# RWKV inverse on one core: the block products of both tiles of a batch taken phase by phase instead of tile by tile

## Chip, cores and metric

One core of a Trainium2 chip. The metric is the device time of one execution in microseconds, as the median over runs; the kernel before was timed three times (1305.89, 1308.43 and 1310.21 us, median 1308.43).

## What is computed

One decoder layer with three token mixers (Mamba-2 SSD, S5, RWKV-7) that read one input projection, are gated, merged, projected and normalised. Batch 1, 256 tokens, model width 2048, all float32.

```python
proj = jnp.einsum('bsd,dc->bsc', x, w_in[l]).astype(jnp.float32)
y_a = mamba2_branch(...)          # SSD, 32 heads
y_b = s5_branch(...)              # complex diagonal scan
y_c = rwkv7_branch(...)           # 16 heads of 64 channels
gates = jax.nn.sigmoid(p_gate.reshape(b, s, N_BRANCHES, d) + gate_b[l])
merged = gates[:, :, 0] * (y_a @ w_branch_a[l]) + gates[:, :, 1] * (y_b @ w_branch_b[l]) + gates[:, :, 2] * (y_c @ w_branch_c[l])
x = layer_norm(DEEPNORM_ALPHA * x + merged @ w_out[l], ln_g[l], ln_b[l])
# inside rwkv7_branch, for every token t and head:
state = state * w_t[:, :, None, :] + sa[..., None] * b_t[:, :, None, :] + v_t[..., None] * k_t[:, :, None, :]
y_t = jnp.einsum('bhvk,bhk->bhv', state, r_t)      # sa = state @ a_t
```

## The kernel before

Every projection is done to nearly float32 precision by splitting both factors in a high and a low part (fp32r): per block of 128 input channels three matmuls of 128x256, `xhi*hi`, `xlo*hi` and `xhi*lo` (lines 417 to 419 for the input projection, 1234 to 1236 for the branches, 863 to 865 and 1337 to 1339 with 512 columns). They are called weight matmuls here. Each weight tile is loaded by DMA, rounded to `hi` on ScalarE (L344), and `lo = raw - hi` is made on VectorE (L346). These weight matmuls stream through TensorE for nearly the whole kernel, and everything else on TensorE is put between them in small groups. Such a group, from the last weight matmul before it to the first one after it, is called a visit.

The RWKV recurrence is done in chunks of 64 tokens, 4 chunks, for 4 batches of 2 tiles of 2 heads each (`b` 0 to 3; tile `i`, head `h`, chunk `c`). Each chunk needs the inverse of a 64x64 unit triangular matrix. Its two 32x32 diagonal blocks are inverted on VectorE (`rwkv_tinv`, L676 and L677, 31 column steps) and go through DRAM into `TTf` (L685). The off-diagonal block is made from them by two products, and this is the part that the change touches:

- `rwkv_ty1` (L698) transposes one diagonal block of both tiles, 16 matmuls of 32x32, into PSUM tiles `py`.
- `rwkv_ty2` copies it to `Y` on ScalarE (L709), multiplies by `Aoff` (L712), copies (L713), multiplies by the other diagonal block (L716), and copies the result into `TTf` (L717). It does so tile by tile, and inside a tile half by half: L712 of one head, its copy, L712 of the other head, its copy, then the same with L716. `Y` has one buffer.
- `rwkv_chunks` then walks the 4 chunks of a batch in order: L731 (a product that needs no inverse), copy, L735 (multiplies by `TTf`), copy, L741, L744 and L747.

A float32 matmul is two instructions in the trace, so a group of 4 matmuls of 32x32 is eight there.

The program order is written in two lists of steps (`PROG`: `T` is the diagonal inverse, `Y` the products, `C` the chunks; `PROG2` after it, with `S` an SSD group and `s` an S5 tile). A scheduler that simulates the engines makes from it the fixed order of instructions on each engine; a step whose inputs come earlier is placed earlier. SSD group work touched below: L924 and L927 are the two matmuls of the state tile `st`, with the ScalarE copy `ST` (L926) between them, and L942 is the product `y`. S5: L1143 makes `s5pk`, ScalarE copies it in four pieces (L1147), and L1195 (`s5y`) uses the copy; L1173 makes `s5bu`.

Of the kernel before, what the change touches and what calls it, by code (L numbers as in the profile page):

```python
# [8 lines left out]
F32 = mybir.dt.float32  # L9
F32R = mybir.dt.float32r  # L10
AF = mybir.ActivationFunctionType
# [193 lines left out]
def emit(tc, I, O, parts=("rwkv", "s5", "ssd", "final"), dbg=None):  # L205
    nc = tc.nc
    ctx = ExitStack()
    with ctx:
# [23 lines left out]
        for st in PROG:  # L232
            if st[0] in "FAB":
                b = int(st[1:])
                if st[0] != "B":
                    bts[b] = rwkv_keys(g, b)
                if st[0] != "A":
                    rwkv_front(g, bts[b], b)
            elif st[0] == "T":
                rwkv_tinv(g, bts[int(st[1:])], int(st[1:]))  # L240
            elif st[0] == "Y":
                b = int(st[1:])
                with tc.high_priority() if b in BEHIND else ExitStack():
                    with tc.issue_after(g.mms[BEHIND[b][0]][BEHIND[b][1]].ins) if b in BEHIND else ExitStack():
                        py = rwkv_ty1(g, bts[b], b)
                    rwkv_ty2(g, bts[b], b, py)
            elif st[0] == "C":
                with tc.high_priority() if int(st[1:]) in BEHIND else ExitStack():
                    rwkv_chunks(g, bts[int(st[1:])], int(st[1:]))
            elif st[0] == "g":  # L250
                gate_c(g, int(st.split("_")[1]))
            elif st[0] == "z":
                rwkv_z(g, int(st[1:]))
            else:
                s5_u(g, int(st[1:]))
# [188 lines left out]
NCH = T // CL  # L444
# [217 lines left out]
def rwkv_tinv(g, bt, b):  # L662

    nc, rp = g.nc, g.rp
    AT = rp.tile([128, 32, 32], F32, name=f"AT{b}", tag="AT")
    TT = rp.tile([128, 8, 32], F32, name=f"TT{b}", tag="TT")
    Pm = rp.tile([128, 8, 32], F32, name=f"Pm{b}", tag="Pm")
    src = bt.Ad.rearrange("i c h q s t -> (i c h q) s t")
    for cs in range(4):
        nc.sync.dma_start(AT[32 * cs:32 * cs + 32], src)  # L670
    nc.sync.dma_start(TT.rearrange("p c i -> p (c i)"), g.I["tti"])
    nc.gpsimd.memset(AT.rearrange("p s t -> p (s t)")[:, ::33], 1.0)  # L672
    for i in range(1, 32):
        n = i + 1
        col = AT[:, 0:n, i].unsqueeze(1).to_broadcast([128, 8, n])
        nc.vector.tensor_tensor(Pm[:, :, 0:n], TT[:, :, 0:n], col, ALU.mult)  # L676
        nc.vector.tensor_reduce(TT[:, :, i], Pm[:, :, 0:n], AX.X, ALU.add)  # L677
    for cs in range(4):
        r = slice(32 * cs, 32 * cs + 32)
        nc.sync.dma_start(bt.Td[:, cs], TT[r])  # L680
    td = bt.Td.rearrange("(m h q) u c i -> m h q (u c) i", h=2, q=2)
    for h in range(2):
        for q in range(2):
            r0 = 64 * h + 32 * q
            nc.sync.dma_start(bt.TTf[r0:r0 + 32, h].rearrange("s i c t -> s (i c) t")[:, :, 32 * q:32 * q + 32],  # L685
                              td[:, h, q].rearrange("m c i -> c m i"))


HS = [(slice(64 * h, 64 * h + 32), slice(64 * h + 32, 64 * h + 64)) for h in range(2)]
# [11 lines left out]


def rwkv_ty2(g, bt, b, pys):
    nc, rp = g.nc, g.rp
    for i in range(2):
        py = pys[i]
        Y = rp.tile([128, 2, NCH, 32], F32, name=f"Yl{b}_{i}", tag="Yl", bufs=1)
        for lo, hi in HS:
            nc.scalar.activation(Y[lo, 0], py[lo, 0], AF.Copy)  # L709
        for lo, hi in HS:  # L710
            for c in range(NCH):
                nc.tensor.matmul(py[hi, 1, c, :], lhsT=bt.Aoff[lo, i, c, :], rhs=Y[lo, 0, c, :], start=True, stop=True)  # L712
            nc.scalar.activation(Y[hi, 1], py[hi, 1], AF.Copy)  # L713
        for h, (lo, hi) in enumerate(HS):
            for c in range(NCH):
                nc.tensor.matmul(py[lo, 2, c, :], lhsT=Y[hi, 1, c, :], rhs=bt.TTf[hi, h, i, c, 32:64], start=True, stop=True)  # L716
            nc.scalar.activation(bt.TTf[lo, h, i, :, 32:64], py[lo, 2], AF.Copy)  # L717


def rwkv_chunks(g, bt, b):  # L720
# [669 lines left out]
```

## Time and profile before

| | |
|---|---|
| median of 3 runs | 1308.43 us (1305.89 to 1310.21) |
| the profiled execution | 1302.54 us, span of the instructions 1300.6 us |
| granted TensorE clock, mean | 0.997 |
| TensorE matmul busy | 1268.7 us (98%) |
| VectorE busy | 995.7 us (77%) |
| ScalarE busy | 768.5 us (59%) |

The profiled execution is 5.9 us below the median of the runs. "Busy" for TensorE means that some matmul was in flight; it doesn't say that the matmuls stood as close as they can, so a visit that spreads them out is inside the 98%.

### The profile page before, as it was taken

Reading aid. Unit: us, or ns where it says so; the run is one execution under the profiler, and the core shown is the slowest. Engines: PE = TensorE matmul, PEld = TensorE weight load, DVE = VectorE, ACT = ScalarE, POOL = GpSimd, SP = SyncE. Lnnn points to the kernel's source line nnn. Section 1 sums busy time; section 2 is a strip of 40 time slices with the busy share of each in tenths; the row PEclk is TensorE's granted clock in tenths of the full one; section 3 lists DMA queues with packets and bytes.
Section 4 is the critical chain, followed back from the end, with each engine's and each line's share of the span. In section 5 each row is a group of like instructions: output and inputs, shape, how many; then the busy total and the mean of one; then the engine's idle time right before and its main releaser. Section 6 shows DMA issues by size and latency. Waiting matters only on the chain.

```text
span 1300.6 us, 27378 instructions
## 1 busy us (share of the span) xinstructions
PE 1268.7 (98%) x10916; PEld 1195.2 (92%) x10916; DVE 995.7 (77%) x1823; ACT 768.5 (59%) x1379; POOL 14.8 (1%) x72
## 2 busy tenths in 40 slices
PE   8999999999999999989999999999999999999996
PEld 8999999999989889889989989999999999999885
DVE  6779987669959857889999867999597565448655
ACT  6676555577555657885756766766454454444530
POOL 2000000000000000000000000000000000000000
PEclk9999999999999999999999999999999999999998
DMA  8655655444564554555555556456655656677751
GB/s 313 181 169 173 187 174 167 139 124 145 166 177 152 168 183 132 159 186 164 178 163 180 170 178 195 146 158 192 193 171 164 193 179 211 209 230 243 255 167 65
DMA packets 97039, 230.71 MB, mean 177 GB/s; under 512 B 26736, under 2 KB 41616, under 8 KB 96912
## 3 DMA queue, kind: packets, MB, share of 16 engines
q1 hardware_dynamic: 96336, 227.60, 57.1%
q8 instruction: 86, 1.41, 0.5%
q10 hardware_dynamic: 576, 1.36, 0.3%
q14 instruction: 41, 0.34, 0.1%
HBM read 224.37 MB, written 3.24 MB: 175 GB/s over the span
## 4 chain that ended last, share of the span: by engine, by line
PE 80%; DVE 7%; ACT 6%; DMA 3%; issue 2%; SPq 1%; DVEq 0%; POOL 0%; ACTq 0%; POOLq 0%
PE ps_g L418 6%; PE ps_g L417 6%; PE ps_g L419 6%; PE br L1235 4%; PE br L1234 4%; PE br L1236 4%; PE ps_x L417 3%; PE ps_x L418 3%; PE ps_x L419 3%; PE po L1337 2%; PE po L1338 2%; PE po L1339 2%; PE zq L865 2%; PE zq L864 2%; PE zq L863 2%
## 5 line engine op out<-in xcount | busy, mean ns | idle before, releaser
L417 PE MATMUL ps_g<-xhi,hi_g 128*128 128x256 f32 x768 | 215.2, 280 | 0.0
L418 PE MATMUL ps_g<-xlo,hi_g 128*128 128x256 f32 x768 | 215.1, 280 | 0.0
L419 PE MATMUL ps_g<-xhi,lo_g 128*128 128x256 f32 x768 | 213.8, 278 | 0.0
L346 DVE TENSOR_TENSOR lo_g<-raw_g,hi_g 128x1024 fp32r<-128x1024 f32 x96 | 117.5, 1224 | 66.6 <-ACT hi_g L344 61.9
L344 ACT ACTIVATE hi_g<-raw_g 128x1024 fp32r<-128x1024 f32 x96 | 101.5, 1058 | 93.8 <-PE ps_g L418 71.4
L418 PEld LDWEIGHTS ps_g<-xlo,hi_g 128*128 128x128 f32 x768 | 144.6, 188 | 2.0 <-issue 1.0
L417 PEld LDWEIGHTS ps_g<-xhi,hi_g 128*128 128x128 f32 x768 | 144.6, 188 | 0.9
L417 PE MATMUL ps_x<-xhi,hi_x 128*128 128x256 f32 x512 | 144.6, 282 | 0.6 <-ACT sq L950 0.6
L419 PEld LDWEIGHTS ps_g<-xhi,lo_g 128*128 128x128 f32 x768 | 144.2, 188 | 0.5
L418 PE MATMUL ps_x<-xlo,hi_x 128*128 128x256 f32 x512 | 143.9, 281 | 0.0
L419 PE MATMUL ps_x<-xhi,lo_x 128*128 128x256 f32 x512 | 143.6, 280 | 0.0
L344 ACT ACTIVATE hi_b<-raw_b 128x1024 fp32r<-128x1024 f32 x64 | 67.8, 1059 | 75.8 <-PE br L1235 43.9
L346 DVE TENSOR_TENSOR lo_x<-raw_x,hi_x 128x1024 fp32r<-128x1024 f32 x64 | 78.3, 1223 | 27.1 <-ACT hi_x L344 27.1
L417 PEld LDWEIGHTS ps_x<-xhi,hi_x 128*128 128x128 f32 x512 | 96.3, 188 | 1.6 <-ACT sq L950 0.8
L419 PEld LDWEIGHTS ps_x<-xhi,lo_x 128*128 128x128 f32 x512 | 96.3, 188 | 0.9 <-issue 0.2
L418 PEld LDWEIGHTS ps_x<-xlo,hi_x 128*128 128x128 f32 x512 | 96.3, 188 | 0.7 <-issue 0.2
L346 DVE TENSOR_TENSOR lo_b<-raw_b,hi_b 128x1024 fp32r<-128x1024 f32 x64 | 78.8, 1231 | 21.6 <-ACT hi_b L344 19.6
L344 ACT ACTIVATE hi_x<-raw_x 128x1024 fp32r<-128x1024 f32 x64 | 67.5, 1055 | 39.7 <-PE ps_x L418 23.2
L1234 PE MATMUL br<-yh0h,hi_b 128*128 128x256 f32 x256 | 72.0, 281 | 0.7 <-DVE sg L1297 0.7
L1235 PE MATMUL br<-yh0l,hi_b 128*128 128x256 f32 x256 | 72.3, 283 | 0.0
L1236 PE MATMUL br<-yh0h,lo_b 128*128 128x256 f32 x256 | 71.7, 280 | 0.0
L676 DVE TENSOR_TENSOR Pm<-TT,AT 128x16 f32<-128x16 f32 (+30 forms) x124 | 50.8, 410 | 11.6 <-POOL AT L672 5.8
(446 smaller groups left out, 3872.9 us busy)
## 6 DMA issues: line engine op xcount, KB each, us to landing
raw_g<-in_wt SPq DMA_DIRECT2D x96, 512.0 KB, 4.4
raw_x<-in_wt SPq DMA_DIRECT2D x64, 512.0 KB, 4.2
raw_za<-in_wza SPq DMA_DIRECT2D x32, 512.0 KB, 3.8
raw_b<-in_wba SPq DMA_DIRECT2D x32, 512.0 KB, 4.5
raw_wo<-in_wout SPq DMA_DIRECT2D x32, 512.0 KB, 4.7
raw_k<-in_wt SPq DMA_DIRECT2D x16, 512.0 KB, 4.8
raw_r<-in_wt SPq DMA_DIRECT2D x16, 512.0 KB, 4.1
raw_v<-in_wt SPq DMA_DIRECT2D x16, 512.0 KB, 3.8
```

The lines of the kernel that those rows point to most:

```text
L344: nc.scalar.activation(hi, raw, AF.Copy)
L346: nc.vector.tensor_tensor(lo, raw, hi.bitcast(F32), ALU.subtract)
L417: m.append(nc.tensor.matmul(ps, lhsT=hi.k(k), rhs=g.xhi[:, k, :], start=(k == 0), stop=False))
L418: m.append(nc.tensor.matmul(ps, lhsT=hi.k(k), rhs=g.xlo[:, k, :], start=False, stop=False))
L419: m.append(nc.tensor.matmul(ps, lhsT=lo.k(k), rhs=g.xhi[:, k, :], start=False, stop=(k == NK - 1)))
L676: nc.vector.tensor_tensor(Pm[:, :, 0:n], TT[:, :, 0:n], col, ALU.mult)
L863: nc.tensor.matmul(ps[tk], lhsT=g.xhi[:, kk, t], rhs=hi.k512(k), start=f0, stop=False)
L864: nc.tensor.matmul(ps[tk], lhsT=g.xhi[:, kk, t], rhs=lo.k512(k), start=False, stop=False)
L865: nc.tensor.matmul(ps[tk], lhsT=g.xlo[:, kk, t], rhs=hi.k512(k), start=False, stop=l0)
L1234: nc.tensor.matmul(ps, lhsT=hi.k(k0 + k), rhs=h, start=(k == 0), stop=False)
L1235: nc.tensor.matmul(ps, lhsT=hi.k(k0 + k), rhs=l, start=False, stop=False)
L1236: nc.tensor.matmul(ps, lhsT=lo.k(k0 + k), rhs=h, start=False, stop=(k == n - 1))
```

## The change

`rwkv_ty2` takes both tiles through each phase together: the copies of `Y` for both, all 16 matmuls of the first product, the four copies, all 16 of the second product, the four copies. The two heads alternate inside a phase. The second tile's `Y` gets a buffer of its own, from the ring `sq2` of two buffers that the z step (`zt`, L783) and the chunk's tail (`ysq`, L766) use. No matmul or copy is added or removed. Lines after L717 move by 6 (L731 becomes L737, L735 L741, L924 L930, L927 L933, L942 L948, L1143 L1149, L1173 L1179, L1195 L1201); L712 becomes L713, L713 becomes L716, L716 becomes L720 and L717 becomes L723.

```diff
 def rwkv_ty2(g, bt, b, pys):
+
     nc, rp = g.nc, g.rp
+    Ys = [rp.tile([128, 2, NCH, 32], F32, name=f"Yl{b}_{i}", tag=("Yl", "sq2")[i], bufs=1 + i) for i in range(2)]
     for i in range(2):
-        py = pys[i]
-        Y = rp.tile([128, 2, NCH, 32], F32, name=f"Yl{b}_{i}", tag="Yl", bufs=1)
         for lo, hi in HS:
-            nc.scalar.activation(Y[lo, 0], py[lo, 0], AF.Copy)
+            nc.scalar.activation(Ys[i][lo, 0], pys[i][lo, 0], AF.Copy)
+    for i in range(2):
+        for c in range(NCH):
+            for lo, hi in HS:
+                nc.tensor.matmul(pys[i][hi, 1, c, :], lhsT=bt.Aoff[lo, i, c, :], rhs=Ys[i][lo, 0, c, :], start=True, stop=True)
+    for i in range(2):
         for lo, hi in HS:
-            for c in range(NCH):
-                nc.tensor.matmul(py[hi, 1, c, :], lhsT=bt.Aoff[lo, i, c, :], rhs=Y[lo, 0, c, :], start=True, stop=True)
-            nc.scalar.activation(Y[hi, 1], py[hi, 1], AF.Copy)
+            nc.scalar.activation(Ys[i][hi, 1], pys[i][hi, 1], AF.Copy)
+    for i in range(2):
+        for c in range(NCH):
+            for h, (lo, hi) in enumerate(HS):
+                nc.tensor.matmul(pys[i][lo, 2, c, :], lhsT=Ys[i][hi, 1, c, :], rhs=bt.TTf[hi, h, i, c, 32:64], start=True, stop=True)
+    for i in range(2):
         for h, (lo, hi) in enumerate(HS):
-            for c in range(NCH):
-                nc.tensor.matmul(py[lo, 2, c, :], lhsT=Y[hi, 1, c, :], rhs=bt.TTf[hi, h, i, c, 32:64], start=True, stop=True)
-            nc.scalar.activation(bt.TTf[lo, h, i, :, 32:64], py[lo, 2], AF.Copy)
+            nc.scalar.activation(bt.TTf[lo, h, i, :, 32:64], pys[i][lo, 2], AF.Copy)
```

The scheduler makes a new order from this. ScalarE, batch 2, from the first copy of `Y` on, before (`py_0` and `Yl_0` are tile 0's; tile 1's copies stand in the same pattern behind these rows):

```order
L709 ACTIVATE Yl_0_4896<-py_0_4878 32x128 x2
L344 ACTIVATE hi_u_1_5479<-raw_u_1_5477 128x1024
L560 ACTIVATE acc_248<-ps_g_10_5359,hgb 128x256
L832 ACTIVATE ea<-par 32x1
L713 ACTIVATE Yl_0_4896<-py_0_4878 32x128
L344 ACTIVATE hi_u_0_5535<-raw_u_0_5533 128x1024
L713 ACTIVATE Yl_0_4896<-py_0_4878 32x128
L344 ACTIVATE hi_u_1_5541<-raw_u_1_5539 128x1024
L971 ACTIVATE yb<-ps_u_5421 128x128x2
L815 ACTIVATE dtu<-dtx 32x256
L816 ACTIVATE dtu<-dtu 32x256
L717 ACTIVATE TTf_2625<-py_0_4878 32x4x32
```

The same place after the change:

```order
L709 ACTIVATE Yl_0_4896<-py_0_4878 32x128 x2
L709 ACTIVATE Yl_1_4897<-py_1_4887 32x128 x2
L344 ACTIVATE hi_u_0_5473<-raw_u_0_5471 128x1024
L716 ACTIVATE Yl_0_4896<-py_0_4878 32x128 x2
L716 ACTIVATE Yl_1_4897<-py_1_4887 32x128 x2
L344 ACTIVATE hi_u_1_5479<-raw_u_1_5477 128x1024
L560 ACTIVATE acc_248<-ps_g_10_5359,hgb 128x256
L723 ACTIVATE TTf_2625<-py_0_4878 32x4x32 x2
L723 ACTIVATE TTf_2625<-py_1_4887 32x4x32 x2
```

Both tiles' copies now stand together, and no copy of a tile waits behind the other tile's products.

TensorE, batch 1, the first product, as a piece of the difference (weight matmuls of a z tile around it):

```order
+L713 MATMUL py_0_2560<-Yl_0_2578,Aoff_1160 32x32 x8
 L419 MATMUL ps_z_3466<-xhi,lo_z_0_3458 128x256
 L417 MATMUL ps_z_3466<-xhi,hi_z_0_3456 128x256
 L418 MATMUL ps_z_3466<-xlo,hi_z_0_3456 128x256
 L419 MATMUL ps_z_3466<-xhi,lo_z_0_3458 128x256
+L713 MATMUL py_1_2569<-Yl_1_2579,Aoff_1160 32x32 x8
```

In batches 1 and 3 the first product is thus two visits, four weight matmuls apart; in batches 0 and 2 it is one, and the second product (L720) is one in all four.

TensorE, SSD group 2 (an early step of `PROG2`), before (`st` is the group's state; L927, its second matmul, follows thirteen weight matmuls after the last row):

```order
L924 MATMUL st_7324<-xdec_7322,BT_7306 128x256
L418 MATMUL ps_x_7452<-xlo,hi_x_0_7442 128x256
L419 MATMUL ps_x_7452<-xhi,lo_x_0_7444 128x256
L417 MATMUL ps_x_7452<-xhi,hi_x_0_7442 128x256
L418 MATMUL ps_x_7452<-xlo,hi_x_0_7442 128x256
L419 MATMUL ps_x_7452<-xhi,lo_x_0_7444 128x256
L942 MATMUL y_7344<-xdt_7315,csb_2_7298 128x64 x4
L942 MATMUL y_7344<-xdt_7315,csb_2_7300 128x64 x4
```

The same group after the change:

```order
L930 MATMUL st_7324<-xdec_7322,BT_7306 128x256
L948 MATMUL y_7344<-xdt_7315,csb_2_7298 128x64 x4
L948 MATMUL y_7344<-xdt_7315,csb_2_7300 128x64 x4
L1149 MATMUL s5pk_7822<-s5cq_7798,s5W_7793 32x32 x8
L1179 MATMUL s5bu_0_7886<-s5U_7784,s5WT_7820 128x128 x3
L933 MATMUL st_7324<-ST_7326,C_7139 128x256
L1179 MATMUL s5bu_0_7886<-s5U_7784,s5WT_7820 128x128
L1201 MATMUL s5y_7918<-yb,s5k_5882 128x128
```

The first S5 tile's work has come forward into the same visit, and no weight matmul stands between the two matmuls of `st`, nor between `s5pk` and `s5y`.

## Rows read from the trace of the kernel before

**Rows 1.** The page: busy time of each engine, and the chain by engine.

```profile
PE 1268.7 (98%) x10916; PEld 1195.2 (92%) x10916; DVE 995.7 (77%) x1823; ACT 768.5 (59%) x1379; POOL 14.8 (1%) x72
...
PE 80%; DVE 7%; ACT 6%; DMA 3%; issue 2%; SPq 1%; DVEq 0%; POOL 0%; ACTq 0%; POOLq 0%
```

**Rows 2.** Waits of TensorE: waiting line and releaser; us in total, times, longest us.

```profile
PE yT L959 <- ACT y L955: 4.1, 5, 1.3
PE py L698 <- DMA TTf<-Td: 4.1, 4, 1.7
...
PE st L927 <- ACT ST L926: 2.7, 1, 2.7
PE chy L744 <- ACT SVA L737: 1.8, 1, 1.8
...
PE s5pb L1137 <- DVE yb L1201: 0.2, 1, 0.2
```

**Rows 3.** TensorE in order of time, a lone visit of eight (start us, us).

```profile
170.84 0.28 PE L417 MATMUL ps_r<-xhi,hi_r 128*128 128x256 f32 x1
...
171.18 0.28 PE L417 MATMUL ps_r<-xhi,hi_r 128*128 128x256 f32 x1
171.38 0.43 PE L712 MATMUL py<-Yl,Aoff 32*32 32x32 f32 x8
171.75 0.39 PE L418 MATMUL ps_r<-xlo,hi_r 128*128 128x256 f32 x1
...
172.33 0.28 PE L419 MATMUL ps_r<-xhi,lo_r 128*128 128x256 f32 x1
```

**Rows 4.** TensorE in order of time, the 32 instructions of L698 in one visit.

```profile
236.92 0.28 PE L418 MATMUL ps_k<-xlo,hi_k 128*128 128x256 f32 x1
237.13 0.69 PE L698 MATMUL py<-cst,TTf 32*32 32x32 f32 x32
237.75 0.39 PE L419 MATMUL ps_k<-xhi,lo_k 128*128 128x256 f32 x1
...
238.32 0.28 PE L417 MATMUL ps_k<-xhi,hi_k 128*128 128x256 f32 x1
```

**Rows 5.** TensorE in order of time, a visit shared with a chunk's product.

```profile
181.67 0.28 PE L419 MATMUL ps_g<-xhi,lo_g 128*128 128x256 f32 x1
181.87 0.45 PE L731 MATMUL ch<-SVA,XS 128*64 128x64 f32 x8
182.25 0.43 PE L712 MATMUL py<-Yl,Aoff 32*32 32x32 f32 x8
182.62 0.38 PE L417 MATMUL ps_g<-xhi,hi_g 128*128 128x256 f32 x1
...
183.19 0.28 PE L418 MATMUL ps_g<-xlo,hi_g 128*128 128x256 f32 x1
```

**Rows 6.** TensorE in order of time, one matmul of L735 as a visit.

```profile
195.33 0.28 PE L418 MATMUL ps_g<-xlo,hi_g 128*128 128x256 f32 x1
195.53 0.33 PE L735 MATMUL ch<-X,TTf 128*64 128x64 f32 x2
195.79 0.38 PE L419 MATMUL ps_g<-xhi,lo_g 128*128 128x256 f32 x1
...
196.13 0.28 PE L418 MATMUL ps_g<-xlo,hi_g 128*128 128x256 f32 x1
```

**Rows 7.** ScalarE's copies by line: duration ns min/median/max, first and last start.

```profile
L709 ACT ACTIVATE Yl<-py x16: 249/268/269, 164.1 to 465.8; 32x128 f32<-32x128 f32 x16
...
L1147 ACT ACTIVATE s5k<-s5pk x32: 168/188/190, 600.5 to 990.8; 32x32 f32<-32x32 f32 x32
```

**Rows 8.** Stretches: length, then PE, PEld, DVE, ACT, POOL busy us, PEclk, DMA share, GB/s.

```profile
480.00:520.00 40.00, 38.87 (x381) 36.74 (x382) 30.16 (x57) 29.37 (x69) 0.00 (x0) 1.00 0.51 158
...
560.00:600.00 40.00, 34.36 (x288) 33.42 (x286) 38.90 (x119) 29.93 (x55) 0.21 (x2) 1.00 0.49 154
```

**Rows 9.** ScalarE in order of time, ahead of the copy `ST` at 565.90.

```profile
564.07 1.28 ACT L937 ACT_TABLE_LOAD   x1
```

## The prediction

> **What bounds the kernel now.** I read the page first. TensorE is busy 98% of the span, VectorE 77%, ScalarE 59%, and the chain of work that ended last runs through TensorE for 80% of the span [rows 1]. Next, TensorE's own waits. There are 13 of them and they add up to 21.4 us, the largest two 4.1 us each [rows 2]. So of 1300.6 us TensorE stands still for under 2%. It is the bound, and what can be gained in quantity is either those 21 us or work of TensorE itself. The third view, TensorE in order of time, shows where its own time can be lost without a wait. In a plain stretch the weight matmuls start 0.113 us apart (three steps from 170.84 to 171.18) [rows 3]. A visit of small matmuls breaks this pace by more than its own arithmetic, and that is the quantity the change works on.
>
> **What a visit costs.** Take the last weight matmul before the visit and the fifth after it: five steps at 0.113 would be 0.567 us. Around a lone L712 group of eight they are 172.33 - 171.18 = 1.15, so the visit costs 0.58 us [rows 3]. Around 32 instructions of L698 they are 238.32 - 236.92 = 1.40, so it costs 0.83 us [rows 4]; with the odd hundredth that still lags behind I take 0.85. Four times the matmuls cost 0.27 us more: most of a visit is its fixed part. Where L712 shares the visit of a chunk's product the two together cost 183.19 - 181.67 - 0.57 = 0.95 [rows 5]; with 0.58 for one of them, sharing costs about 0.38. A single matmul of L735 alone costs, over four steps, 196.13 - 195.33 - 0.34 = 0.46, say 0.47 [rows 6].
>
> **The change, part by part.**
>
> Removed: by the order, the products of L712 and L716 are 32 groups of eight before, eight per batch. 19 of them are visits of their own and 13 share one with other small work: 19 x 0.58 + 13 x 0.38 = 16.0 us. Beside that, in every batch the first L735 is torn into three pieces, since the second tile's inverse comes late; three pieces at 0.47 against one whole visit of 0.58 is 0.8 us, four times 3.3 us. Together 19.3 us.
>
> Added: six full visits of 32 (four L720, two L713) and, in batches 1 and 3, the first product in two visits of 16 instructions each, which lie between 0.58 and 0.85; I take 0.67. That is 6 x 0.85 + 4 x 0.67 = 7.8 us. One L731 in batch 0 is torn in two instead (2 x 0.47 - 0.58 = 0.4). Together 8.2 us. **The visits save 19.3 - 8.2 = 11 us**, all on TensorE and so on the path.
>
> The price of a full visit is the one unknown here, since no L712 or L716 group of 32 exists. From below it is L698's 0.83, the nearest row: the same 32x32 shape, 32 instructions, both heads alternating as the new loops do. From above it is four groups that each pay the price of sharing, 0.20 + 4 x 0.38 = 1.7 us, as if nothing overlapped; then two halves cost 0.96 each, the added part is 14.4 us, and 5 us are saved. I take the lower one. Against it stands a rule of the Trainium skill (TensorE: Matmul & The Clock Gate, section "Wait — 56ns, not 53.3ns?"): start-to-start of matmuls never drops below about 25 ns, however few columns they have. By an estimate from that page a visit of 32 would be at least 31 x 9 ns = 0.28 us dearer than I say and six of them 1.7 us. The trace doesn't agree: 32 instructions, each 0.19 us long, fit in 0.69 us, which is 16 ns apart [rows 4].
>
> Copies: sixteen of each kind, each about 0.27 us [rows 7], are the same number on ScalarE as before, now four in a row. TensorE's next phase waits for four instead of one or two: 4 x 0.27 = 1.1 us. In the order 21 to 29 weight matmuls, 2.4 us or more, stand ahead of each phase; only behind the second half of the first product in batches 1 and 3 they are 16 and 18, and its own two copies take 0.54. So nothing is added there while those weight matmuls are ready; without them each of the eight phases would show 1.1 us. One more table load on ScalarE (42 for 41, 1.28 us [rows 9]) lies beside other work. Rounding of weights that is queued on ScalarE behind a copy waits for the visit at most once per phase rather than twice per tile; it has slack (59%).
>
> Moved: the end of the chunks. Counted in weight matmuls, the last chunk's matmuls of batch 0 move from about 1625 to 1511, of batch 1 from 2079 to 1825, of batch 3 from 3447 to 3152, so at 0.113 us each 13, 29 and 33 us earlier. No TensorE work disappears with that; it only frees VectorE and ScalarE work of the recurrence to be done earlier, and pulls S5's first tile forward (its first matmul from weight matmul 3830 to 3662). From 480 to 520 us VectorE is busy 30.2 of 40 us, from 560 to 600 it is 38.9 of 40, and there TensorE has only 34.4 [rows 8]. DMA issues are the same in number; the four groups that carry the inverse through DRAM move with it on SP's queue, and weight loads behind them have not held TensorE so far (no weight load is among the waits of rows 2).
>
> Waits: the one I expect to get longer is at SSD group 2. There ScalarE's copy `ST` came 2.7 us late once [rows 2], behind table loads of 1.28 us [rows 9], although 18 weight matmuls (2.0 us) stood between the two matmuls of `st`. In the new order none stand there, and four copies of 0.19 us [rows 7] also lie uncovered between `s5pk` and `s5y` in the same visit. Bounds: nothing, if other work in that visit or an earlier ScalarE covers it; 2.7 + 2.0 + 0.8 = 5.5 us. I take 3. Of the other waits I drop half of the 1.8 us before L744 [rows 2], since its place and ScalarE's order both change. Net **2 us more waiting**.
>
> Sum: -11 + 2 = -9 us. The profiled execution would go from 1302.5 to 1293.5; it stands 5.9 us below the median of the runs shown, so for the median I say 1308.4 - 9.4, or 1299.
>
> **The rivals.** (1) The early end of the chunks also takes waits away. For it: the stretch from 560 us, where VectorE is full and TensorE loses 5.6 us [rows 8], gets its S5 work earlier out of a stretch with 10 us of idle VectorE. Against it: the new order itself packs S5's tile into one visit with group 2. If all of those 5.6 us and the 1.8 go, and the visit at group 2 is covered, it is 1308.4 - 11 - 7.4 = 1290. (2) The visits are worth less: full visits near 1.7 us, or phases that wait for their four copies, 8 x 1.1 us. Saved 5 us, less 2 of waiting: 1305, which is no change. For it: the operands come from SBUF places that ScalarE has only just written; against it: L698 also multiplies blocks that have just arrived, at 0.83. (3) Slower: the one visit of group 2 and S5's first tile becomes a long halt. Six dependent steps stand in it without a weight matmul, and TensorE takes its instructions in order, so everything waits for the latest of `ST`, `s5k` and the S5 weights, and all three are made by ScalarE. It decides from 15 us on, since it must eat the 11 us and 4 more. ScalarE would need about four table loads (5.1 us) and ten instructions of 1 us ahead of them; before, the halt at this copy was 2.7 us. At 18 us it gives 1308 - 11 + 18 = 1315. (4) That the change doesn't do what it says is excluded by the order for the second product, and half true for the first in batches 1 and 3, which is in the sum.
>
> **How the numbers follow.** A measurement of this kernel tells about 0.3%, 3.9 us, from no change. My forecast has 0.62, rival 1 0.13, rival 2 (with forecasts in which the waits eat most of the gain) 0.17, rival 3 0.08. So faster 0.75, within 0.3% 0.17, slower 0.08. The range runs from rival 1 (1290) to forecasts with visits at 1.7 us and the full 5.5 us of waiting, 1308.4 - 5 + 5.5 = 1309; I give 1289 to 1309.
>
> **What would show it.** Right: L713 and L720 as groups of 32 (two of 16) with the fifth weight matmul about 1.4 us behind the last one before; L741 whole in every first chunk; the chunks' last matmuls of batch 3 some 30 us earlier; sum of TensorE's waits near 23 us. Wrong: a full visit over 1.2 us; L713 or L720 waiting for L709 or L716 by name; a wait at `st`, `s5y` or `s5bu` of over 5 us; or waits that sum to over 30 us.

## The result and the profile after

| | before | after |
|---|---|---|
| median | 1308.57 us (1305.89 to 1310.21, 4 runs) | 1294.45 us (1293.05 to 1295.61, 4 runs) |
| profiled execution | 1302.54 us, span 1300.6 | 1294.02 us, span 1292.0 |
| granted TensorE clock, mean | 0.997 | 0.992 |

The ratio is 0.9894, with a 95% interval of 0.9874 to 0.9913: 14.1 us faster, between 11.4 and 16.5. The two profiled executions are only 8.5 us apart. The text below takes these two differences apart.

The page of after, its first lines on the engines, the granted clock in 40 slices, and the chain by engine:

```profile
PE 1264.8 (98%) x10916; PEld 1193.6 (92%) x10916; DVE 994.7 (77%) x1823; ACT 769.0 (60%) x1380; POOL 15.0 (1%) x72
...
PEclk9999989999999999899999999999999999999999
...
PE 87%; DVE 5%; ACT 3%; DMA 2%; issue 2%; SPq 1%; ACTq 0%; DVEq 0%; POOL 0%; POOLq 0%
```

The same instructions ran on TensorE, 10916, and it is busy 3.9 us less than in [rows 1]. It is still the bound. Its share of the chain rose from 80% to 87%, that of VectorE and ScalarE fell from 13% to 8%. The two slices with an 8 in the clock row are new; they come up again below.

The visits first. TensorE of after in order of time (start us, us): a second product with all 32 instructions in one visit, batch 0.

```profile
173.48 0.28 PE L419 MATMUL ps_r<-xhi,lo_r 128*128 128x256 f32 x1
173.69 0.69 PE L720 MATMUL py<-TTf,Yl 32*32 32x32 f32 x32
174.31 0.39 PE L417 MATMUL ps_r<-xhi,hi_r 128*128 128x256 f32 x1
...
174.77 0.28 PE L417 MATMUL ps_r<-xhi,hi_r 128*128 128x256 f32 x1
```

Over four steps it costs 174.77 - 173.48 - 4 x 0.113 = 0.84 us, as L698 does in [rows 4], and all four L720 visits lie between 0.840 and 0.843. The same view in batch 1 shows the first product in its two halves:

```profile
226.68 0.28 PE L418 MATMUL ps_z<-xlo,hi_z 128*128 128x256 f32 x1
226.89 0.44 PE L713 MATMUL py<-Yl,Aoff 32*32 32x32 f32 x16
...
227.93 0.44 PE L713 MATMUL py<-Yl,Aoff 32*32 32x32 f32 x16
...
228.75 0.28 PE L417 MATMUL ps_z<-xhi,hi_z 128*128 128x256 f32 x1
```

From 226.68 to 228.75 there are eight steps of weight matmuls, so the two halves cost 2.07 - 0.91 = 1.16 us, 0.58 each. Sixteen alternating instructions cost no more than a lone eight (0.58 in [rows 3]).

Waits of TensorE, after (waiting line and releaser; us in total, times, longest us):

```profile
PE zq L870 <- DVE lo_za L346: 3.6, 1, 3.6
PE warm L360 <- ACT zero L358: 3.2, 1, 3.2
PE py L698 <- DMA TTf<-Td: 2.3, 2, 1.2
PE py L713 <- ACT Yl L709: 1.5, 1, 1.5
PE yT L965 <- ACT y L961: 1.4, 1, 1.4
...
PE zq L869 <- ACT hi_za L344: 0.9, 1, 0.9
...
```

With those under 0.15 us, which the view leaves out, they add up to 16.7 us, against 21.5 of before. The 2.7 us at `st` behind `ST` and the 1.8 us before L744 are gone [rows 2], and so are three waits of the branch matmuls (L1234, 3.1 us together in before); `yT` fell from 4.1 to 1.4 and L698 from 4.1 to 2.3. L713 with 1.5 us and a `ps_u` matmul with 1.0 are new, and `zq` rose from 0.4 to 4.5 us.

The three stretches behind the end of the chunks, by windows (us, then busy time and count of PE, PEld, DVE, ACT and POOL, granted clock, DMA share, GB/s), after:

```profile
480.00:520.00 40.00, 39.29 (x327) 38.44 (x326) 35.67 (x74) 29.36 (x56) 0.00 (x0) 1.00 0.61 179
520.00:560.00 40.00, 35.48 (x188) 30.05 (x187) 30.81 (x101) 26.88 (x41) 0.11 (x1) 0.91 0.45 136
560.00:600.00 40.00, 39.10 (x342) 37.93 (x341) 39.21 (x84) 29.82 (x68) 0.32 (x3) 1.00 0.63 189
```

The last chunk matmul (L747, now L753) starts at 479.2 us instead of 527.0, and VectorE's idle time from 480 us is used: 35.7 us busy for 30.2 [rows 8]. TensorE's 5.6 idle us from 560 us are down to 0.9. But the stretch ahead of it, which had none in before, now has 4.5.

### The profile page after: what moved, and what is told of

It reads as the page before. It is cut to its first block, busy times and chain, and to the rows that moved or that the text cites. A ratio compares the mean times of both kernels' runs of the same rounds, so it can differ in the third digit from the quotient of the medians.

```text
span 1292.0 us, 27378 instructions
## 1 busy us (share of the span) xinstructions
PE 1264.8 (98%) x10916; PEld 1193.6 (92%) x10916; DVE 994.7 (77%) x1823; ACT 769.0 (60%) x1380; POOL 15.0 (1%) x72
## 4 chain that ended last, share of the span: by engine, by line
PE 87%; DVE 5%; ACT 3%; DMA 2%; issue 2%; SPq 1%; ACTq 0%; DVEq 0%; POOL 0%; POOLq 0%
PE ps_g L419 7%; PE ps_g L418 7%; PE ps_g L417 7%; PE br L1241 5%; PE br L1240 5%; PE br L1242 5%; PE ps_x L417 4%; PE ps_x L419 4%; PE ps_x L418 4%; PE po L1345 2%; PE po L1344 2%; PE po L1343 2%; PE zq L870 2%; PE zq L871 2%; PE zq L869 2%
```

## What the two profiles add up to

The span can be split from the starts of the weight matmuls. Every step from one weight matmul to the next that is longer than the pace (0.113 us, 0.22 with 512 columns) has an excess. I took the waits out of it, as the trace records them, and gave the rest to the visit if one lies in the step or fewer than five steps back; the excess of all other steps that fall into a stretch at half the granted clock (1.2 GHz instead of 2.4) is the clock's. For this split every matmul of 128x128 by 256 or 512 columns counts as a weight matmul. What then remains is the pace itself, with small jitter, and the two ends. The number of visits stands in brackets. The last column differs by up to 3.8 us between executions, and this split doesn't say why, so a difference of that size between two rows is not to be read from it.

| kernel (profiled execution) | span | visits | TensorE's waits | half clock outside visits | the rest |
|---|---|---|---|---|---|
| before | 1300.6 | 150.8 (179) | 21.5 | 0 | 1128.3 |
| before, another execution | 1306.5 | 152.3 (179) | 22.2 | 4.5 | 1127.5 |
| after | 1292.0 | 139.1 (171) | 16.7 | 4.9 | 1131.3 |
| after, another execution | 1291.6 | 138.5 (171) | 20.2 | 5.1 | 1127.8 |
| before with `Y` in two buffers | 1305.9 | 145.6 (173) | 25.1 | 3.9 | 1131.3 |
| both heads in one visit | 1288.7 | 143.4 (173) | 16.5 | 0.7 | 1128.1 |
| the same, another execution | 1294.3 | 143.9 (173) | 19.6 | 1.9 | 1128.9 |

The visits fell by 150.8 - 139.1 = 11.7 us between the first two profiles and by 152.3 - 138.5 = 13.8 between the other two; forecast were 11. Waits fell by 4.8 and 2.0. The execution of before that the prediction was summed against is the only one of these seven that loses nothing at half clock, and this is the larger part of why the first two profiles lie closer together than the medians: -11.7 of visits, -4.8 of waits, +4.9 at half clock, +3.0 of the rest. The other pair is 14.9 us apart, near the 14.1 of the medians: -13.8 of visits, -2.0 of waits, +0.6 at half clock, +0.3 of the rest.

How such a stretch looks: TensorE of after, batch 0, behind two waits for the transfer of the inverse (in brackets the idle time before and its releaser):

```profile
161.33 0.22 PE L698 MATMUL py<-cst,TTf 32*32 32x32 f32 x2 [1.06 <-DMA TTf<-Td]
162.78 1.06 PE L698 MATMUL py<-cst,TTf 32*32 32x32 f32 x30 [1.23 <-DMA TTf<-Td]
...
164.36 0.41 PE L419 MATMUL ps_v<-xhi,lo_v 128*128 128x256 f32 x1
...
168.84 0.41 PE L419 MATMUL ps_v<-xhi,lo_v 128*128 128x256 f32 x1
```

Here the weight matmuls start 0.213 us apart (164.36 to 168.84 in 21 steps) instead of 0.113. At that pace a stretch of 6.83 us loses 6.83 x (1 - 0.113 / 0.213) = 3.2. The windows of the same ten microseconds, first after, then the second execution of before, then the second of after, each a view of its own:

```profile
160.00:170.00 10.00, 7.71 (x92) 7.13 (x90) 5.13 (x11) 3.35 (x7) 0.15 (x1) 0.66 0.50 135
```

```profile
160.00:170.00 10.00, 8.02 (x72) 7.66 (x73) 5.79 (x13) 3.36 (x6) 0.15 (x1) 0.66 0.54 140
```

```profile
160.00:170.00 10.00, 7.79 (x117) 7.29 (x116) 4.70 (x8) 5.77 (x12) 0.15 (x1) 1.00 0.55 153
```

A clock of 0.66 over 10 us is 6.8 us at half. In the third row TensorE stood just as long (2.2 us at L698 in two waits, against 2.3 in the first) and kept its clock. So this stretch belongs neither to the change nor to the place; the wait at L698 is in both kernels and is followed by one in some executions.

The other stretch of after, 6.83 us behind the `zq` waits, is not of that kind. It stands in all five traces whose other instructions keep the change's order (the two of after and the three with added matmuls below), from 529.6 to 534.7 us and 6.83 us long each time, and in neither trace of the version without that halt (the heads alone, below). The timed runs say the same: the ten of the changed kernel have mean granted clocks of 0.990 to 0.994 (mean 0.992), the 58 of before beside the experiments 0.990 to 0.998 (mean 0.994), the nine of the heads alone 0.993 to 0.997 (mean 0.995). As one stretch of 6.83 us takes 0.0026 from the mean clock and costs 3.2 us, the changed kernel loses by estimate some 3 us more at half clock than the kernel before.

## The experiments

The kernels ran in three groups, each beside runs of the kernel before. Its median was 1306.81 us (29 runs) beside the first four below, 1306.84 (19 runs) beside the added matmuls and the heads, and 1308.19 (10 runs) beside the last three.

**The kernel before, again.** No edit; a second profile.

> The kernel before, unchanged, to see the granted clock of each timed execution. Profiled execution of before: 1302.5 us at a mean clock of 0.997, timed runs 1305.9 to 1310.2. If the timed runs have stretches at half clock that the profiled one lacks (one stretch of 6.8 us at half clock costs up to 3.4 us and 0.0026 of the mean clock), the runs at 1306 to 1310 show 0.990 to 0.995. If the clock is 0.997 in all of them, the 6 us between profile and median have another cause.

Measured: 1306.62 us (1304.48 to 1310.89, 11 runs), ratio 0.9996 (0.9987 to 1.0006). The profiled execution took 1308.43 us and has stretches at half clock behind L698 (161.8 us), `yT` (513.4) and `ST` (571.4). Its single runs had mean clocks of 0.991 to 0.997. What follows: 1302.5 us was an unusually short execution to sum against, and of the 5.9 us between the two profiles 4.5 are half clock outside visits.

**The transposes of batch 0 later, in the kernel before and in the kernel after.** One number of the order; the transposes of L698 are held until weight matmul 41 of the fifth `v` tile instead of 23.

```diff
-BEHIND = {0: ("v4", 23), 2: ("g2_11", 47)}
+BEHIND = {0: ("v4", 41), 2: ("g2_11", 47)}
```

> Before, with the transposes of batch 0 (L698) queued 18 weight matmuls later, so that the blocks have arrived from DRAM. The 1.7 us wait there and any half-clock stretch behind it should go. If the wait alone counts: 2 us less (ratio 0.9985). If a half-clock stretch follows this wait in most timed runs: 5 us less (0.996). If it is covered anyway: no change. The chunks of batch 0 end where they did.

> The changed kernel with the same delay of L698 of batch 0. Its trace has 2.3 us of waits there and 6.8 us at half clock behind them. Against before: 0.989 if neither counts, 0.9875 if the waits alone go, 0.985 if the half-clock stretch goes too (1294.4 - 2.3 - 3.4 = 1288.7). The second half-clock stretch, behind the wait of the zq matmuls at 535 us, should stay.

Measured: before so delayed 1307.36 us (12 runs), ratio 1.0005 (0.9991 to 1.0019); after so delayed 1292.16 us (1289.02 to 1295.01, 4 runs), ratio 0.9874 (0.9856 to 0.9893), whose interval overlaps that of the change itself. The waits of the delayed kernel before show where the time went (same columns as above):

```profile
PE py L698 <- DMA TTf<-Td: 3.2, 3, 1.3
...
PE py L716 <- ACT Yl L713: 1.7, 1, 1.7
```

L698 fell from 4.1 to 3.2 us, and 1.7 us came up at L716, which had none in the first profile of before (1.1 us in the second). The delay moves the wait; it doesn't remove it.

**Only the buffer.** The loops of before, with the second tile's `Y` in the ring that the change uses. The second tile's products may then run among the first's, and by the order the 32 groups lie in 20 visits, the first L735 of a batch is whole, and the chunks of batch 3 end some 200 weight matmuls earlier. Two things that the change does are thus half done, without its loops.

```diff
-        Y = rp.tile([128, 2, NCH, 32], F32, name=f"Yl{b}_{i}", tag="Yl", bufs=1)
+        Y = rp.tile([128, 2, NCH, 32], F32, name=f"Yl{b}_{i}", tag=("Yl", "sq2")[i], bufs=1 + i)
```

> Before with the second buffer for Y alone, loops as before. In its order the two tiles go through the phases side by side: 20 visits instead of 32, no torn L735, chunks of batch 3 end about 200 weight matmuls (23 us) earlier, in the change 292. If the visits carry the gain: the products' visits cost 4x0.58 and 16x0.63... in all 12 us against 19.3 before and 8.2 in the change, so 7 us are gained of the change's 11, ratio near 0.9945 before what waits and clock do. If the early end of the chunks carries it: nearly all of the 14 us, ratio 0.990.

Measured: 1307.06 us (1303.78 to 1311.68, 11 runs), ratio 1.0001 (0.9987 to 1.0014). Its visits are 5.2 to 6.7 us cheaper in the table, and it gained nothing. Its waits:

```profile
PE yT L959 <- ACT y L955: 6.8, 2, 3.8
PE s5y L1195 <- ACT s5k L1147: 3.9, 1, 3.9
...
```

They sum to 25.1 us, 3.6 more than before. The wait at `s5y` is the place of rival 3: ScalarE's `s5k` late in front of the first S5 tile, 3.9 us. Behind it the pace halves (TensorE in order of time):

```profile
575.99 0.76 PE L1195 MATMUL s5y<-yb,s5k 128*128 128x128 f32 x2 [3.89 <-ACT s5k L1147]
...
576.76 0.41 PE L418 MATMUL ps_x<-xlo,hi_x 128*128 128x256 f32 x1
576.98 0.41 PE L419 MATMUL ps_x<-xhi,lo_x 128*128 128x256 f32 x1
```

Half clock takes its part too: its eleven runs have mean clocks of 0.988 to 0.993 (mean 0.990), lower than those of before, and its profile has four stretches of 3.4 us ahead of the last ten microseconds. So an early end of the chunks is by itself no gain, and a new order that saves 5 to 7 us of visits can lose them again in waits and half-clock stretches that nobody placed. How much each of them took is not shown: against the second profile of before the waits are 2.9 us longer, half clock takes 0.6 less, and 3.8 us lie in the rest.

**The price of a visit by itself.** The next three kernels add 112 spare matmuls of 32x32, whose result nothing reads, to the last 14 gate tiles of the changed kernel. The order is otherwise the same and the number of matmuls too; only the grouping differs: 28 lone visits of 4 matmuls of one head, or 7 visits of 16 with the heads alternating, or 7 visits of 16 with one head behind the other (the three lines below in this order).

```diff
+PLACES, EVERY, GROUP = (14, 32), 0, [(0, 0, c) for c in range(4)]
+PLACES, EVERY, GROUP = (14,), 2, [(i, h, c) for i in range(2) for c in range(4) for h in range(2)]
+PLACES, EVERY, GROUP = (14,), 2, [(i, h, c) for h in range(2) for i in range(2) for c in range(4)]
...
+        with g.tc.high_priority(), g.tc.issue_after(m[at].ins):
+            for i, h, c in GROUP:
+                lo, hi = HS[h]
+                nc.tensor.matmul(g.dmt[hi, i, c, :], lhsT=idn[lo, lo], rhs=idn[lo, lo], start=True, stop=True)
```

> The changed kernel with 112 more 32x32 matmuls into a spare part of PSUM that nothing reads, in 28 lone visits of 4 between the weight matmuls of the last 14 gate tiles (about 990 to 1150 us), where TensorE waits for nothing. All other instructions keep their order. If a visit costs by itself, as in the prediction: 28 x 0.58 = 16.2 us more than the changed kernel, about 1310. If only the matmuls count (112 x 2 instructions at 16 ns): 3.6 us more, about 1298, and the same as in the two runs beside it.

> The same 112 matmuls in 7 visits of 16, the two heads' blocks alternating as in the change. By the price of a visit: 7 x 0.84 = 5.9 us more than the changed kernel, about 1300, and 10.3 us less than with 28 lone visits. If only the matmuls count: 3.6 us more, as with the lone ones.

> The same 7 visits of 16, first all matmuls of one head's block and then all of the other's, as the loops before had them. If alternating blocks matters (8 instructions of one block take 0.43 us, 34 ns apart, 32 alternating ones 0.69, 16 ns apart), a visit costs 0.5 + 32 x 0.034 = 1.4 instead of 0.84 us: 9.6 us more than the changed kernel. If not: as the run before, 5.9.

Measured, with ratios to the kernel before; the changed kernel at its ratio of 0.9894 would stand at 0.9894 x 1306.84 = 1293.0 beside these:

| | median | ratio | over 1293.0 | sum of its visits in its trace |
|---|---|---|---|---|
| 28 lone | 1309.18 (12 runs) | 1.0016 (1.0002 to 1.0029) | 16.2 | 28 x 0.581 = 16.3 |
| 7 alternating | 1298.43 (5 runs) | 0.9934 (0.992 to 0.9948) | 5.4 | 7 x 0.841 = 5.9 |
| 7 head by head | 1302.32 (8 runs) | 0.9965 (0.995 to 0.9981) | 9.3 | 7 x 1.241 = 8.7 |

The alternating visit reads as that of L720 above, 0.69 us from its first start to its last end. The other two, TensorE in order of time; alone:

```profile
1068.46 0.28 PE L427 MATMUL ps_g<-xhi,lo_g 128*128 128x256 f32 x1
1068.67 0.43 PE L1288 MATMUL dmt<-cst 32*32 32x32 f32 x8
1069.03 0.39 PE L425 MATMUL ps_g<-xhi,hi_g 128*128 128x256 f32 x1
```

head by head:

```profile
1090.38 0.28 PE L427 MATMUL ps_g<-xhi,lo_g 128*128 128x256 f32 x1
1090.59 1.09 PE L1288 MATMUL dmt<-cst 32*32 32x32 f32 x32
1091.61 0.39 PE L425 MATMUL ps_g<-xhi,hi_g 128*128 128x256 f32 x1
```

In all three the first matmul of a visit starts 0.21 us behind the last weight matmul; then 8 instructions take 0.43 us, 32 alternating 0.69 and 32 head by head 1.09. Same work, a third of the price: **such a visit is paid by the visit, and it costs in the timed runs what it costs in the trace.** (By its interval and that of the base, each time over 1293.0 is good to some 3 us.) That the last two differ, in the traces and by intervals that just don't overlap, shows a second thing: alternating heads are part of the gain. Read with the first two, 24 more instructions cost 0.26 us if heads alternate and 0.66 if they don't.

Which visits pay the fixed part can be read from the changed kernel itself. S5's L1201 is one matmul over the whole array, two instructions of 128 columns. TensorE of after in order of time:

```profile
806.94 0.28 PE L419 MATMUL ps_zb<-xhi,lo_zb 128*128 128x256 f32 x1
807.05 0.38 PE L1201 MATMUL s5y<-yb,s5k 128*128 128x128 f32 x2
...
807.75 0.28 PE L418 MATMUL ps_zb<-xlo,hi_zb 128*128 128x256 f32 x1
```

It starts 0.11 us behind the last weight matmul instead of 0.21, and over five steps the visit costs 807.75 - 806.94 - 0.567 = 0.24 us, 0.12 for each instruction. One matmul with a weight block of 128x64, half the array, and only 64 columns costs 0.47 [rows 6]. Over the whole trace of after the first instruction of a visit starts, in the median, 0.12 us behind the last weight matmul of 256 columns where its weight block is 128x128 (95 visits) and 0.205 to 0.21 where it is smaller (94 visits of seven shapes). So not every visit pays the fixed part: in this kernel those pay it whose blocks use a part of the array.

The Trainium skill (TensorEngine Tiling (Array Packing), Key Properties) has a reason for the fixed part: changing the tiling mode drains TensorE, while different tiles can load and multiply in parallel. The rows agree with both halves: a fixed part near half a microsecond for blocks on a part of the array and none for L1201, which has the shape of the weight matmuls around it, and blocks on different parts of the array that overlap. That the drain is what takes the half microsecond is not shown by itself. Of the 25 ns floor that the prediction weighed, from the page TensorE: Matmul & The Clock Gate, nothing is seen in the alternating visit: (0.69 - 0.19) / 31 = 16 ns apart.

**Only the heads together.** The loops over heads and chunks swapped as in the change, but the tiles one after the other and `Y` in its one buffer: 16 product groups by the order in place of 10; in the trace seven of them share a visit with chunk products.

```diff
-        for lo, hi in HS:
-            for c in range(NCH):
+        for c in range(NCH):
+            for lo, hi in HS:
                 nc.tensor.matmul(py[hi, 1, c, :], lhsT=bt.Aoff[lo, i, c, :], rhs=Y[lo, 0, c, :], start=True, stop=True)
+        for lo, hi in HS:
             nc.scalar.activation(Y[hi, 1], py[hi, 1], AF.Copy)
...
```

> Before with one visit a phase for both heads of a tile, tiles still one after the other and Y with one buffer. In its order the products are 16 groups, 8 or 9 of them lone, and L735 is torn less; chunks of batch 3 end 264 weight matmuls earlier. By visits: about 10 us of them against 19.3 before and 8.2 in the change, so 9 us saved, ratio 0.993, plus or minus what waits and half-clock stretches do (the run with the second buffer alone saved 5 us of visits and lost them again to 4 us more waits). If the early end of the chunks decides: no gain, as with the second buffer alone, which ended them 203 earlier and gained nothing.

Measured: 1292.43 us (1290.61 to 1294.13, 4 runs), ratio 0.9896 (0.9882 to 0.9911), the same as the change. That is some 5 us better than the forecast by visits (0.993). Its visits cost 4 to 5 us more than those of the change in the table; it makes up some 3 of them, by estimate, at half clock, since it has no long halt at `zq` (waits of 1.0 and 0.6 us there) and no stretch behind it.

**The change, the heads alone, and the heads alone with the later transposes, on the same runs.**

> The changed kernel as it is, a second time, beside the two kernels below and the same runs of the kernel before. If the change's part beyond the visits (about 3 of its 14 us) lies in waits of TensorE and in stretches at half the granted clock that come and go from execution to execution, the ratio stays near 0.989 within 0.002, but the profile shows other half-clock stretches than the first one did (162.69 and 534.74, 6.83 us each), while the visits keep their prices to 0.01 us: L720 0.84 each, L713 in halves 0.63. If the stretches belong to fixed places of the changed order, both come again at the same places with the same length.

> Both heads in one visit, the tiles one after the other, Y in one buffer (as in the earlier run of this edit, 1292.4 us). If it is the change's equal, it lies within 2 us of the kernel after the change on these same runs, with 16 product groups instead of 10 but without the second buffer. If the earlier 2 us were real, it is faster than the change by about 2 us again.

> The same with the transposes of batch 0 placed 18 steps later, which gave the changed kernel perhaps 2 us (1292.2 for 1294.5) and the kernel before nothing. The order has two more visits (199 for 197) with it, about 1 us. If the wait at L698 of batch 0 and the half-clock stretch behind it cost 3 to 4 us, which the delay takes away, the time is 1290 us. If the wait only moves to another place, as it did in the kernel before, the time is 1293 us.

Measured: the change 1293.51 us (1290.89 to 1295.79, 6 runs), ratio 0.9897 (0.9875 to 0.9919); the heads alone 1294.51 (1290.32 to 1296.32, 5 runs), 0.9892 (0.9868 to 0.9917); the heads with the delay 1292.71 (1290.58 to 1294.96, 5 runs), 0.9889 (0.9868 to 0.9911). The three can't be told apart, and the 2 us by which the heads alone seemed faster did not come again. No version beats the change by what a measurement can tell; the one without the second buffer equals it with less.

In the change's second profile both halves of the expectation come true. One stretch is in the place of the first profile and as long (532.5 us, 6.83 us, behind the `zq` waits), the one behind L698 is not there, and two came up elsewhere, at 10.2 us and at 573.4, in front of which TensorE waited 1.3 us. The L720 visits are 0.84 again, the halves 0.58 and 0.59. (The 0.63 of the expectation had counted part of the second half into the first.) In the delayed version the wait moved to the chunk's first product (L731 of before, here L733; its waits, same columns):

```profile
PE ch L733 <- ACT TTf L719: 2.1, 1, 2.1
...
PE py L698 <- DMA TTf<-Td: 0.8, 1, 0.8
```

## Why the prediction held, and where not

**The visits.** Forecast -11 us from [rows 3 to 6]; measured -11.7 and -13.8 over all visits, other small work that now falls together differently included. The unknown, a full visit, was taken at 0.85 from L698: L720 is 0.84, L713 in batch 0 of the second profile 0.84 (1.02 in the first, where part of it ran at half clock). The sixth, L713 in batch 2, is dearer in both profiles, 1.23 and 1.32 us, because it is torn by its copies (next paragraph): one of the signs of error that the prediction had set, a full visit over 1.2 us, is there. The halves were taken at 0.67 and are 0.58. All first L741 of a batch are whole, at 0.60; L737 is torn once, as the order had it, and one later L741 is torn into six and two instructions, 0.58 + 0.47, which the prediction didn't count. Rival 2, visits near 1.7 us, is refuted by these rows, of which one of six is over 1.2 us; but its upper bound was not absurd, since the same 32 instructions head by head cost 1.24. The diff swaps the loops so that the heads alternate, and this is what makes L698 the right neighbour.

**The copies.** The prediction had them covered by 21 weight matmuls and more. In all but one of the first and second products no wait is seen (in the second profile the chunk's L737 also waited 0.9 us for the copies into `TTf`). In batch 2 there is one, named by the prediction as a sign of error. ScalarE there (with idle time before, and its releaser):

```profile
359.79 1.06 ACT L344 ACTIVATE hi_u<-raw_u 128x1024 fp32r<-128x1024 f32 x1 [3.53 <-DVE dtq L832]
...
361.11 1.10 ACT L709 ACTIVATE Yl<-py 32x128 f32<-32x128 f32 x4
```

and TensorE:

```profile
361.69 1.01 PE L713 MATMUL py<-Yl,Aoff 32*32 32x32 f32 x32 [1.47 <-ACT Yl L709]
```

The four copies take 1.10 us as estimated. They stand behind a rounding and a gate's activation (L560), and ScalarE had stood 3.5 us for VectorE's `dtq`. So L713 waited 1.5 us; in the second profile 0.1. It then started on tile 0's copies while those of tile 1 were still to come, stood again for 0.13 us between the tiles, and its 32 instructions took 1.01 us instead of 0.69, in both profiles. What the step missed is not the copies' own length but that they queue behind an engine that is itself waiting.

**The waits: the term that failed.** Forecast was +2 us net; measured -4.8 and -2.0. The 3 us at SSD group 2 and the first S5 tile did not come: no wait at `ST`, `s5y` or `s5bu` is among those of after. The forecast had taken it that nothing covers the copy `ST`, as no weight matmul stands between the two matmuls of `st`. But the visit's own small matmuls do. TensorE of after at that place:

```profile
567.99 0.59 PE L930 MATMUL st<-xdec,BT 128*128 128x256 f32 x2
568.42 1.89 PE L948 MATMUL y<-xdt,csb 128*128 128x64 f32 x16
...
571.14 0.70 PE L933 MATMUL st<-ST,C 128*128 128x256 f32 x2
```

The two stand 3.2 us apart, filled and without a halt, and `ST` was done at 569.85. ScalarE was late again, but for something else: ScalarE of after ahead of `zq`, an SSD projection,

```profile
523.24 1.28 ACT L1029 ACT_TABLE_LOAD   x1
...
524.90 1.28 ACT L943 ACT_TABLE_LOAD   x1
...
526.85 1.28 ACT L1031 ACT_TABLE_LOAD   x1
...
528.48 1.28 ACT L890 ACT_TABLE_LOAD   x1
...
530.41 1.04 ACT L344 ACTIVATE hi_za<-raw_za 128x1024 fp32r<-128x1024 f32 x1
```

VectorE behind it,

```profile
528.50 0.19 DVE L1035 SCALAR_TENSOR_TENSOR s5pw<-s5t 128x32 f32<-128x32 f32 x1 [3.17 <-ACT s5t L1031]
...
534.59 1.22 DVE L346 TENSOR_TENSOR lo_za<-raw_za,hi_za 128x1024 fp32r<-128x1024 f32 x1
```

and TensorE at the same time:

```profile
531.50 0.73 PE L869 MATMUL zq<-hi_za,xhi 128*128 128x512 f32 x2 [0.89 <-ACT hi_za L344]
535.86 0.79 PE L870 MATMUL zq<-lo_za,xhi 128*128 128x512 f32 x1 [3.62 <-DVE lo_za L346]
```

Four table loads of 1.28 us in a row, as rival 3 wanted, without the ten other instructions that it also wanted. They fell on the split of `za` instead of on the group's copy, and the halt was 4.5 us, not 18. Only 0.9 of it is ScalarE's rounding. The other 3.6 us TensorE waited for VectorE's `lo_za`: the rounding had ended at 531.45, but VectorE, which had stood 3.2 us for ScalarE's S5 function behind the table loads, first worked off eighteen small instructions of S5 and SSD and began `lo_za` at 534.59. The prediction had ScalarE's table loads and put their delay at one place; it had nothing for the delay that they pass on to VectorE. The place moves with the order, and in this order the halt comes each time (4.5 and 5.4 us in the two profiles, with a stretch at half clock behind it, some 3 us more, for which the prediction had no term either). Rival 3 was wrong in place and in size.

**Rival 1** came half: the 5.6 us of TensorE's idle time from 560 us fell to 0.9 and the wait before L744 went, as it said; but 4.5 us came up from 520 us. Over the three windows TensorE's idle time is 6.8 us before and 6.1 after. That the buffer alone, with its early chunks, gained nothing says the same: the early end does take waits away there too (none at L744, 0.5 us for `ST`, 0.2 at the branches), but others came up for them (`yT` 6.8, `s5y` 3.9), so the early end is not where the gain is. The waits that did shrink lie at L698, `yT`, L744 and `ST`, 9.0 us together, and 5.6 more came up at L713 and `zq`; single waits differ between two executions of the changed kernel by 1 us and a little more (`zq` L869 0.9 and 1.8, `yT` 1.4 and 2.2, L713 1.5 and 0.1). Most of this exchange comes again in the second pair of profiles: the same four places lose 9.6 us, the waits of the branch matmuls (3.1 and 2.2 us in before) are gone both times, and `zq` gains 4.1 and 5.0. So the exchange belongs to the new order; how much of the net 2 to 5 us is chance of the execution stays open.

**The base.** The sum was carried over to the median by keeping the 5.9 us offset of the profiled execution. That offset was not a constant: after's profiled execution lies 0.4 us below its median. What the profile of before couldn't show was that its runs usually hold stretches at half clock. Both kernels have them, and the 8.5 us between the first profiles and the 14 between the medians only agree when they are counted. Of the 14.1 us some 12 to 14 are the visits; the waits give 2 to 5 more, and the stretch behind `zq`, some 3 us by estimate, takes about as much back. So the median came out 5 us below the forecast of 1299 because the visits gave 1 to 3 us more than forecast and the waits had the wrong sign, while the clock, which had no term, went the other way: that the waits and the clock, neither of them forecast rightly, nearly cancel is luck, and what the prediction has by its own working is the 11 us of visits.

**Small slips in the working.** The 13 waits of TensorE are 13 lines of the view; they hold 21 waits, and the longest is the 3.2 us at the start, not 4.1. The price of a piece of L735 is read over three steps, not four; 0.47 stands. The sum carries 9.4 to the median where its terms give 9.0. And the early end of the chunks in batch 3 came to 48 us instead of 33, as the working priced the 295 weight matmuls between and not the visits among them.

## What to carry to other kernels

Small matmuls whose blocks use only a part of the array, put between long streams of whole-array matmuls, are paid by the visit (here near 0.5 us going in and out), not by the matmul: gather what is ready into one visit, and inside it alternate the blocks that use different parts of the array. Take the price from a neighbouring visit of the same shape in the trace, but forecast waits of a newly made order only as a spread (here between -5 and +4 us over the orders tried): they move with the order, and with one edit that saved 5 to 7 us of visits the time stayed the same. Before summing against one profiled execution, look at its granted clock beside those of several runs.

## What the runs showed of the hardware that was not expected

Waits of one to four microseconds in a TensorE that is 98% busy are followed, in some executions, by 3.4 or 6.8 us at half the granted clock; the same wait in another execution isn't. Before's first profile has waits of 2.7 us (`ST`) and 1.7 us (L698) [rows 2] with none behind them, its second profile has one behind each. The halt of 4.4 to 5.4 us at `zq` had one behind it in all five traces of the changed order. A halt can thus cost more than its own length. In this kernel that is a part of the spread from run to run: the 58 runs of before beside the experiments lie between 1302.5 and 1311.6 us, and the longer ones have the lower mean clock (correlation -0.67).

Sixteen instructions of 32x32 with alternating heads cost 0.58 to 0.59 us as a visit, as much as eight of one head alone (0.58), and sixteen of which the second eight are the other head's cost 0.84 (`Y` in two buffers): the second head's instructions come for nothing only where they alternate with the first's.
